# Queries and keys of three head pairs by seven products of halves, with residual tokens and finished heads kept in DRAM

## The chip, the core and the metric

The kernel runs on one core of a Trainium2 chip. A core has engines with instruction streams of their own: TensorE (PE) multiplies, VectorE (DVE) and ScalarE (ACT) work elementwise, GpSimd (POOL) and SyncE (SP) here mostly issue transfers. They meet through semaphores; each engine takes its instructions in the order in which the program has them. Matmul results land in PSUM banks of 2 KB per partition, everything else is in SBUF or DRAM. The metric is the device time of one execution in microseconds, here the median of the runs. The profiler took one execution in detail; its span (first to last instruction) is a little shorter than its measured time.

## The reference, cut to what matters

A model of two layers on 512 tokens of width 1024: dilated window attention and a SwiGLU block, then an mLSTM mixer and a SwiGLU block. The change touches the attention layer alone:

```python
def dilated_attention_mixer(xn, positions, w_in, w_out):
    proj = (xn @ w_in).reshape(B, S, N_GROUPS, 3, ATTN_HEADS, ATTN_HEAD_DIM)   # 3 groups, 8 heads of 128
    for g, (window, dilation) in enumerate(DIL_CONFIGS):                       # (128,1) (512,4) (2048,16)
        q = apply_partial_rope(proj[:, :, g, 0], positions) * scale            # rope on 32 of 128 features
        k = apply_partial_rope(proj[:, :, g, 1], positions)
        v = proj[:, :, g, 2]
        o, lse = dilated_window_attention(q, k, v, window, dilation)
    wts = jax.nn.softmax(jnp.stack(lses), axis=0)
    o = jnp.einsum('gbsh,gbshd->bshd', wts, jnp.stack(outs))
    return o.reshape(B, S, ATTN_WIDTH) @ w_out
```

All is fp32. With xn the normalised input, the queries and keys of one pair of heads in one group are xn times 2 x 256 columns of w_in.

## The kernel before

**Products.** TensorE multiplies in a rounded fp32 form, so each fp32 operand is split into a high part (rounded) and a low part (the rest), and each product is three matmuls: high by high, high by low, low by high (the list SPLITS). The normalised input lies in `pair[0]` (high) and `pair[1]` (low), eight tiles of 128 features by 512 tokens each.

**Weights.** A chunk of 4 x 128 rows by 256 columns (512 KB) is loaded on the SP queue into one of three "wraw" tiles; ACT writes its high part (line 210), DVE its low part (line 211), into three tiles each. `Feed` (line 263) keeps two chunks prepared ahead of the one that TensorE is using: `pop` hands out one and prepares the next of the list `plan`.

**Projections.** `project_pair` goes over groups g = 0, 1, 2 and over queries and keys. `project` (with `multiply`, line 241) gives each projection 48 matmuls 128x512: two chunks, two heads m, four k, three splits. ACT then copies 32 rows of the result to a `rot` tile (line 800) and the whole to the query or key tile (line 801). `rope` (lines 571 to 586) rotates the four 32-row parts at once on DVE (a shuffle, two products, a sum, each 128x512) and ACT copies them back (line 586).

**Attention.** The eight heads are four pairs, pr = 0 to 3. `attention_pair` makes scores of the first group (`scores0`, lines 642 and 648: masking and maxima on DVE, then exponentials on ACT, line 679), scores of the other two (`scores12`, lines 662 to 665, exponentials line 685), an exchange of maxima and sums across groups (lines 693 to 722, with one matmul, xps), the weighting of the probabilities (lines 730, 733, tensor-scalar on DVE), their transposes by DVE and a round trip to DRAM (line 739 and the tiles pD, pT; POOL queue), and the values (lines 757, 762), whose result ACT copies to `oT` (line 766), the tile "heads" with all eight heads.

**The order.** The work of one pair is laid over the projections of the next by ticks: `advance()` runs after each chunk, `defer(n, fn)` lets fn run n ticks later. RUN_AT = (2, (4, 5, 6, 7, 8), (10, 11), (2, 3, 1)) gives scores12 two ticks into the next pair, the exchange and first weighting at 4, transposes and the second weighting at 5 to 8, values at 10 and 11. So the weighting and transposes of pair pr-1 fall in the second group of pair pr, and the values in its third. `fenced()` and `run` hold the order on TensorE.

**Seven products, where they are already.** Most of the values, in the phase before pair 1, and the feed-forward compute a 2x2 block product with seven half-size products instead of eight (names P1 to P7, in the list ORDER: P1, P5, P2, P6, P7, P3, P4). It needs sums of operand blocks. The token sums S1 and S2 lie in the "heads" tile until the values phase ends, S3 and S4 in tiles of the values phase's own pool (`place`, freed with it). `sum_of` and `split_sum` make them. The residual tokens are the tiles `h` (tag "h"), to which `add_to_h` adds the output projection `awo`, the stage after the last values.

Of the kernel before, what the change touches and what calls it, by code (L numbers as in the profile page):

```python
# [72 lines left out]
def tile_hybrid_dilated_attn_mlstm(  # L73
# [310 lines left out]
    with ExitStack() as actx:  # L384
# [16 lines left out]
        posi = ap.tile([P, SEQ], I32, tag="rt", name="posi", bufs=2)  # L401
# [22 lines left out]
        def rope_tables():  # L424
# [142 lines left out]
        def rope(qk, rot, blocks, js=range(4), direct=False):  # L567

            at = slice(R * js[0], R * (js[-1] + 1))
# [3 lines left out]
            nc.vector.tensor_tensor(sh, sh, sinn[at], op=ALU.mult)  # L573
            if direct:
                for j in js:
                    mine = slice(R * j, R * (j + 1))
                    nc.vector.tensor_tensor(qk[j // 2][:R, j % 2], rot[mine, 0], rot[mine, 1], op=ALU.add)
                return
            nc.vector.tensor_tensor(a, a, sh, op=ALU.add)

            def back():
                for j in js:
# [3 lines left out]
                    nc.scalar.activation(t, part, AF.Copy)  # L586
            return back

        o_all = []

        def o_head(k):
            if not o_all:
                o_all.append(ap.tile([P, HEADS, SEQ], F32, tag="heads", name="oT"))
            return o_all[0][:, k]

        def attention_pair(pr, qks):
# [153 lines left out]
            def values(i, out=None):  # L750
# [30 lines left out]

        def project_pair(pr, qks, then=None):
            nm = "a%d" % pr
            for g in range(3):
# [4 lines left out]
                rot = ap.tile([P, 2, SEQ], F32, tag="rt", name="rot", bufs=2)  # L789
                for part in range(2):  # L790
                    t = tok_tile("%sg%d_%s" % (nm, g, "qk"[part]))

                    def evac(m, acc, t=t, rot=rot, g=g, part=part):
                        mine = rot[R * (2 * part + m):R * (2 * part + m + 1), 0]
                        views = (in_order, by_block) if g == 0 else (lambda x: x,) * 2
                        if pr == 0:
                            nc.vector.tensor_tensor(views[0](t[:, m]), views[1](acc), views[1](rbc), op=ALU.mult)
                            nc.scalar.activation(views[1](mine), views[0](t[:R, m]), AF.Copy)
# [1350 lines left out]
```

## Time and profile before

| | us |
|---|---|
| median of three runs | 1396.8 (1395.97 to 1398.32) |
| the profiled execution | 1396.37 |
| its span | 1394.5 |
| pair 2, first group (queries, keys, scores12 of pair 1 between) | 259.21 to 284.70 |
| pair 2, second group | 284.70 to 306.59 |
| pair 2, scores0, third group and values of pair 1 | 306.59 to 338.21 |
| pair 3, the same | 338.21 to 417.21 |
| values columns of pair 3, scores12, output projection, values of pair 3 | 417.21 to 495.25 |
| feed-forward of layer 0 starts | 495.25 |

The granted TensorE clock of the profiled execution is 0.999. In the lines shown below, a tile's name says where it belongs: a2g1k is pair 2, second group (g counts from 0), keys; `_w`, `_h`, `_l` are a raw chunk and its high and low parts; a1p the probabilities of pair 1; xa the normalised input; f0j the feed-forward of layer 0. Lines are those of the kernel before. A busy time counts instructions in execution, which overlap a little on DVE and ACT; so the distance between two starts is often shorter than one's length.

### The profile page before, as it was taken

What the parts mean: (1) busy time and instruction counts of PE and PEld (TensorE: products, weight loads), DVE (VectorE), ACT (ScalarE), POOL (GpSimd) and SP (SyncE); (2) the same over time, 40 slices, a digit from 0 to 9 for tenths busy, and PEclk for the clock granted to TensorE, in tenths of its full rate; (3) what the DMA queues carried; (4) which work ended last, traced back from release to release, by engine and by line L of the source; (5) the groups of instructions that cost most, each with busy time, mean ns of one, the idle gap of its engine ahead of it and who ended that gap; (6) DMA issues with size and microseconds to landing.
All of it is one profiled execution on the core that took longest, in us unless ns stands there. A gap on an engine that the chain in (4) does not pass through costs nothing. (4 is left out here: it accounts for less than half of the span.)

```text
span 1394.5 us, 21550 instructions
## 1 busy us (share of the span) xinstructions
PE 1379.0 (99%) x8308; PEld 1230.7 (88%) x8308; DVE 1046.9 (75%) x1781; ACT 777.2 (56%) x1280; POOL 156.9 (11%) x228
## 2 busy tenths in 40 slices
PE   9999999999999999999999999999999999999997
PEld 7888888888888889999999998897888899999886
DVE  7758746372638399877888898898858988888887
ACT  6546566455655255544576464785535554458854
POOL 2000011111111000000010110123201230001213
PEclk9999999999999999999999999999999999999999
DMA  7534256455453456233352743324334553335963
GB/s 240 164 121 137 78 166 204 121 161 150 126 169 105 159 146 169 95 122 121 108 157 69 175 115 91 92 76 121 91 119 111 142 181 121 122 110 132 197 166 99
DMA packets 137022, 186.39 MB, mean 134 GB/s; under 512 B 8628, under 2 KB 104436, under 8 KB 136920
## 3 DMA queue, kind: packets, MB, share of 16 engines
q1 hardware_dynamic: 117600, 136.14, 31.2%
q0 software_dynamic: 17664, 47.76, 15.0%
q8 instruction: 65, 1.06, 0.3%
q10 hardware_dynamic: 1656, 1.12, 0.2%
q14 instruction: 37, 0.30, 0.1%
HBM read 163.63 MB, written 18.87 MB: 131 GB/s over the span
## 5 line engine op out<-in xcount | busy, mean ns | idle before, releaser
L1452 POOL DMA_DIRECT2D f1T<-in_ffn_w_out_dram x15 | 17.8, 1186 | 208.7 <-DMA f1P_2w_w<-in_ffn_w_out_dram 136.2
L1427 POOL DMA_DIRECT2D f0S<-in_ffn_w_out_dram x10 | 8.7, 871 | 256.5 <-ACT f0P L1409 170.7
L1984 POOL DMA_DIRECT2D hD<-hB x32 | 21.8, 698 | 68.5 <-DVE hB L1981 68.5
L241 PE MATMUL mo<-n_h,mo_k_l 128*128 128x512 f32 x64 | 25.3, 395 | 0.0
L241 PE MATMUL mo<-n_h,mo_k_h 128*128 128x512 f32 x64 | 25.2, 394 | 0.0
L241 PE MATMUL mo<-n_l,mo_k_h 128*128 128x512 f32 x64 | 25.2, 393 | 0.0
L241 PE MATMUL mwo<-yo_l,mwo_k_h 128*128 128x512 f32 x64 | 25.1, 393 | 0.0
L241 PE MATMUL mqk<-n_h,mqk_k_h 128*128 128x512 f32 x64 | 25.1, 393 | 0.0
L241 PE MATMUL awo<-ao_h,awo_k_h 128*128 128x512 f32 x64 | 25.1, 392 | 0.0
L241 PE MATMUL mqk<-n_l,mqk_k_h 128*128 128x512 f32 x64 | 25.1, 392 | 0.0
L241 PE MATMUL f1j<-n_h,f1j_h 128*128 128x512 f32 x64 | 25.0, 391 | 0.0
L241 PE MATMUL f0j<-n_h,f0j_h 128*128 128x512 f32 x64 | 25.0, 391 | 0.0
L241 PE MATMUL mwo<-yo_h,mwo_k_l 128*128 128x512 f32 x64 | 25.0, 391 | 0.0
L241 PE MATMUL mqk<-n_h,mqk_k_l 128*128 128x512 f32 x64 | 25.0, 390 | 0.0
L241 PE MATMUL f0j<-n_h,f0j_l 128*128 128x512 f32 x64 | 24.9, 390 | 0.0
L241 PE MATMUL f1j<-n_h,f1j_l 128*128 128x512 f32 x64 | 24.9, 390 | 0.0
L241 PE MATMUL awo<-ao_h,awo_k_l 128*128 128x512 f32 x64 | 24.9, 389 | 0.0
L241 PE MATMUL f0j<-n_l,f0j_h 128*128 128x512 f32 x64 | 24.9, 389 | 0.0
L241 PE MATMUL f1j<-n_l,f1j_h 128*128 128x512 f32 x64 | 24.9, 389 | 0.0
L241 PE MATMUL awo<-ao_l,awo_k_h 128*128 128x512 f32 x64 | 24.9, 389 | 0.0
L241 PE MATMUL mwo<-yo_h,mwo_k_h 128*128 128x512 f32 x64 | 24.8, 391 | 0.0
L211 DVE TENSOR_TENSOR v1P_l<-v1W,v1P_h 128x1024 fp32r<-128x1024 f32 x14 | 17.1, 1223 | 9.6 <-ACT v1P_h L210 9.6
(2458 smaller groups left out, 5669.8 us busy)
## 6 DMA issues: line engine op xcount, KB each, us to landing
f0j_w<-in_ffn_w_in_dram SPq DMA_DIRECT2D x17, 512.0 KB, 6.0
f1j_w<-in_ffn_w_in_dram SPq DMA_DIRECT2D x17, 512.0 KB, 5.3
f1T<-in_ffn_w_out_dram POOLq DMA_DIRECT2D x15, 512.0 KB, 7.5
f0hid<-in_ffn_w_in_dram SPq DMA_DIRECT2D x9, 512.0 KB, 5.2
f1hid<-in_ffn_w_in_dram SPq DMA_DIRECT2D x9, 512.0 KB, 5.0
v0W<-in_attn_w_in_dram SPq DMA_DIRECT2D x8, 512.0 KB, 6.0
v1W<-in_attn_w_in_dram SPq DMA_DIRECT2D x8, 512.0 KB, 3.9
awo_k_w<-in_attn_w_out_dram SPq DMA_DIRECT2D x8, 512.0 KB, 3.9
```

The source lines that it names most:

```text
L211: nc.vector.tensor_tensor(lo[:, :n], raw[:, :n], hi[:, :n].bitcast(F32), op=ALU.subtract)
L241: nc.tensor.matmul(acc, whl[a][:, k, m * P:(m + 1) * P], pairs[b][kk], start=(kk == 0 and (a, b) == SPLITS[0]), stop=(kk == nk - 1 and (a, ...
L1427: nc.gpsimd.dma_start(t, src[1][:, ks], accum_op=ALU.add)
L1452: nc.gpsimd.dma_start(view(to), weight_rows(hk * UNITS + u, n), accum_op=ALU.add)
L1984: nc.gpsimd.dma_start(hD[k // 4].rearrange("(b i) x -> i b x", i=R)[:, :, c0:c0 + R], t[R * a_:R * (a_ + 1)])
```

## The change

For pairs 1 to 3 and the groups g = 1 and 2, six units in all, queries and keys together are one 2x2 block product: the halves of the 1024 features, the 256 query and 256 key columns, and the two halves of the tokens. With W11, W12, W21, W22 (feature half; 1 for queries, 2 for keys) and X00 to X11 (token half, feature half), the seven products are

```
P1 = W11 X00      P5 = (W12 - W11) S1          S1 = X10 + X11 blocks of the second token half
P2 = W21 X01      P6 = (W22 - W12 + W11) S2    S2 = S1 - X00
P3 = W22 S4       P7 = (W22 - W12) S3          S3 = X00 - X10
                  P4 = (W21 - W22 + W12 - W11) X11    S4 = X01 - S2
```

Each is 24 matmuls 128x256 (two heads, four k, three splits) against 96 matmuls 128x512 in a unit before. P1 and P2 give the queries of the first token half; u = P1 + P6 is kept (`vu`, with P5), P7 and then P4 are added on in the same bank; the key halves are a bank plus the part of `vu` (line 885 after the change, on DVE). The four weight blocks are loaded once per unit (`load_part`, W11 to a tile of its own), and their differences are made in place on DVE (`prepare_part`); each of the seven is split like any chunk.

So that the token sums live on through the attention layer, S3 and S4 move into the slots of the residual tokens h; these go to DRAM (`keep_tokens`, 8 x 256 KB, POOL queue) early in the kernel and come back (`bring_tokens`, SP queue) in the output projection. S1 and S2 stay in the slot of the heads; finished heads 0 to 5 go to DRAM one by one (`keep_head`) and come back in two loads (`bring_heads`) before the last values. The rope tile is laid out by token halves (its tables too), one tile instead of two; copies to and from it become half-size and twice as many where blocks or 256-token halves are moved.

```diff
-            for c in range(4):
-                s = slice(32 * c, 32 * c + 32)
-                nc.gpsimd.tensor_copy(sinn[:R, c * P:(c + 1) * P], sn[s])
-                nc.gpsimd.tensor_copy(cosn[:R, c * P:(c + 1) * P], cs[s])
-            for i in range(1, 4):
-                for t in (sinn, cosn):
-                    nc.gpsimd.dma_start(t[R * i:R * (i + 1)], t[:R])
+            for to, t in ((sinn, sn), (cosn, cs)):
+                for c in range(4):
+                    nc.gpsimd.tensor_copy(
+                        to[R * (c // 2):R * (c // 2 + 1)].rearrange("p (m s) -> p m s", m=2)[:, :, c % 2 * P:(c % 2 + 1) * P],
+                        t[R * c:R * (c + 1)].unsqueeze(1).to_broadcast([R, 2, P]))
+                nc.gpsimd.dma_start(to[2 * R:], to[:2 * R])
...
             def back():
-                for j in js:
-                    t, part = qk[j // 2][:R, j % 2], rot[R * j:R * (j + 1), 0]
+                for q in range(first, end):
                     if blocks:
-                        t, part = in_order(t), by_block(part)
-                    nc.scalar.activation(t, part, AF.Copy)
+                        for m in range(2):
+                            nc.scalar.activation(turned(qk, q, m, True), packed(rot, q, m, True), AF.Copy)
+                    else:
+                        nc.scalar.activation(halves(qk[q // 2][:R], q % 2), two_m(rot[quarter(q), 0]), AF.Copy)
...
+        oD = dp.tile([HEADS - 2, P, SEQ], F32, name="oD")
+        hD = dp.tile([KC, P, SEQ], F32, name="hD")
...
+        def keep_head(k, op):
+            t = npl.tile([P, SEQ], F32, tag="sq", name="o_keep", bufs=2)
+            nc.scalar.activation(t, op, AF.Copy)
+            nc.gpsimd.dma_start(oD[k], t)
+
+        def bring_heads():
+            t = ap.tile([P, HEADS - 2, SEQ], F32, tag="heads", name="oT")
+            o_all.append(t)
+            for ks in (slice(0, 4), slice(4, 6)):
+                nc.sync.dma_start(t[:, ks], oD[ks].rearrange("k p s -> p k s"))
+
+        def keep_tokens():
+            for k in range(KC):
+                nc.gpsimd.dma_start(hD[k], h[k])
+
+        def bring_tokens():
+            for k in range(KC):
+                h[k] = hp.tile([P, SEQ], F32, tag="h", name="h%d" % k, bufs=KC + 1)
+                nc.sync.dma_start(h[k], hD[k])
...
-                    nc.scalar.activation(o_head(2 * pr + i), op, AF.Copy)
+                    keep_head(2 * pr + i, op)
...
+        def load_part(pr, g, key):
+            if g > 2:
+                return
+            pool_, tag, bufs = (ap2, "wa", 1) if key == "W11" else (wp, "wraw", W_BUFS)
+            t = pool_.tile([P, 1024], F32, tag=tag, name="a%dg%d%s" % (pr, g, key), bufs=bufs)
+            k0, c0 = (int(key[1]) - 1) * 4 * P, g * 3 * D + (int(key[2]) - 1) * D + pr * 256
+            nc.sync.dma_start(four_k(t), w_in[k0:k0 + 4 * P, c0:c0 + 256].rearrange("(k p) n -> p k n", p=P))
+            parts_of.setdefault((pr, g), {})[key] = t
...
+        def prepare_part(pr, g, name):
+            b = parts_of[pr, g]
+
+            def less(out, x, y):
+                nc.vector.tensor_tensor(b[out], b[x], b[y], op=ALU.subtract)
+            src = {"P1": "W11", "P5": "W11", "P6": "W11", "P2": "W21", "P7": "W12", "P3": "W22", "P4": "W21"}[name]
+            if name == "P5":
+                less("W11", "W12", "W11")
+            elif name == "P6":
+                less("W11", "W22", "W11")
+            elif name == "P7":
+                less("W12", "W22", "W12")
+            whl = split_chunk((b[src], 1024, four_k, "a%dg%d%s" % (pr, g, name)))
+            if name == "P7":
+                less("W21", "W21", "W11")
+                for key in ("W11", "W12"):
+                    load_part(pr, g + 1, key)
+            elif name == "P4":
+                for key in ("W21", "W22"):
+                    load_part(pr, g + 1, key)
+            return whl
...
+        def qk_unit(pr, g, qk):
+            nm = "a%dg%d" % (pr, g)
+            last = pr == HEADS // 2 - 1 and g == 2
+            target = {"P1": "c11", "P2": "c11", "P5": "p5", "P3": "p5", "P6": "u", "P7": "u", "P4": "u"}
+            two_m = lambda t: t.rearrange("p (m s) -> p m s", m=2)
+            acc = {}
+            rot = vu = None
+
+            def pack(q, src):
+                nc.scalar.activation(two_m(rot[quarter(q), 0]), src, AF.Copy)
+
+            def finish(name):
+                nonlocal rot, vu
+                if name == "P1":
+                    acc["u"] = acc_tile(nm + "u")
+                    nc.scalar.activation(acc["u"], acc["c11"], AF.Copy)
+                elif name == "P5":
+                    vu = ap.tile([P, 2, SEQ], F32, tag="vu", name=nm + "vu")
+                    nc.scalar.activation(vu[:, 0], acc["p5"], AF.Copy)
+                elif name == "P6":
+                    nc.scalar.activation(vu[:, 1], acc["u"], AF.Copy)
+                elif name in ("P2", "P4"):
+                    th = int(name == "P4")
+                    src = two_m(acc[target[name]])
+                    if th == 0:
+                        rot = ap.tile([P, 2, SEQ], F32, tag="rot", name="rot")
+                    pack(th, src[:R])
+                    nc.scalar.activation(halves(qk[0], th), src, AF.Copy)
+                    if last and th:
+                        rope(qk, rot, False, 1, 2, True)
+                else:
+                    th = int(name == "P7")
+                    out = halves(qk[1], th)
+                    nc.vector.tensor_tensor(out, two_m(acc[target[name]]), two_m(vu[:, 1 - th]), op=ALU.add)
+                    pack(2 + th, out[:R])
+                    if last and th == 0:
+                        rope(qk, rot, False, 0, 1, True)
+                        rope(qk, rot, False, 2, 4, True)
+
+            for n, name in enumerate(ORDER):
+                key = target[name]
+                if name in ("P1", "P5"):
+                    acc[key] = acc_tile(nm + key)
+                whl = feed.pop()
+                with fenced():
+                    for m in range(2):
+                        for k in range(4):
+                            for a, b in SPLITS:
+                                if name in ("P1", "P2", "P4"):
+                                    x_ = pair[b][k + 4 * (name != "P1")][:, HALF * (name == "P4"):HALF * (1 + (name == "P4"))]
+                                else:
+                                    x_ = sum_part(name, b, k)
+                                nc.tensor.matmul(acc[key][:, m * HALF:(m + 1) * HALF], whl[a][:, k, m * P:(m + 1) * P], x_,
+                                                 start=(name in ("P1", "P5") and m == 0 and k == 0 and (a, b) == SPLITS[0]),
+                                                 stop=(m == 1 and k == 3 and (a, b) == SPLITS[-1]), skip_group_check=True)
+                finish(name)
+                if n == 6 and not last:
+                    defer(1, rope(qk, rot, False))
+                if n in (1, 3, 5, 6):
+                    advance()
...
+                if pr and g:
+                    qk.extend(tok_tile("%sg%d_%s" % (nm, g, "qk"[part])) for part in range(2))
+                    qk_unit(pr, g, qk)
+                    continue
...
+                        for th in range(2):
+                            q = 2 * part + th
+                            if pr == 0:
+                                nc.scalar.activation(packed(to, q, m, g == 0),
+                                                     turned((t, t), q, m, g == 0), AF.Copy)
+                            else:
+                                nc.scalar.activation(packed(to, q, m, False), acc[:R, th * HALF:(th + 1) * HALF], AF.Copy)
...
-            S[name] = ([heads_s[:, 2 * (int(name[1]) - 1) + i] for i in range(2)] if name in ("S1", "S2") else
-                       [place("s%d" % (2 * (name == "S4") + i), name + "hl"[i], (P, 4, HALF), F32R) for i in range(2)])
-            nc.scalar.activation(S[name][0], raw, AF.Copy)
-            nc.vector.tensor_tensor(S[name][1], raw, S[name][0].bitcast(F32), op=ALU.subtract)
+            if name in ("S1", "S2"):
+                hi, lo = (heads_s[:, 2 * (int(name[1]) - 1) + i] for i in range(2))
+                nc.scalar.activation(hi, raw, AF.Copy)
+                nc.vector.tensor_tensor(lo, raw, hi.bitcast(F32), op=ALU.subtract)
+                S[name] = [[t[:, k] for k in range(4)] for t in (hi, lo)]
+                return
+            S[name] = [[], []]
+            for i in range(2):
+                hi, lo = (hp.tile([P, 2, HALF], F32R, tag="h", name="%s%s%d" % (name, x, i), bufs=KC + 1) for x in "hl")
+                nc.scalar.activation(hi, raw[:, 2 * i:2 * i + 2], AF.Copy)
+                nc.vector.tensor_tensor(lo, raw[:, 2 * i:2 * i + 2], hi.bitcast(F32), op=ALU.subtract)
+                for a, t in enumerate((hi, lo)):
+                    S[name][a] += [t[:, k] for k in range(2)]
...
+            defer(1, keep_tokens)
...
-                if (pr, g) != (0, 0):
+                if pr and g:
+                    if (part, ch) == (0, 0):
+                        plan += [lambda pr=pr, g=g, name=name: prepare_part(pr, g, name) for name in ORDER]
+                elif pr and (part, ch) == (1, 1):
+                    plan.append(lambda pr=pr: last_plain(pr))
+                elif (pr, g) != (0, 0):
...
+        bring_heads()
...
+            if c == 2:
+                bring_tokens()
```

More of the change, by code (lines that the diff above doesn't have):

```diff
@@ L565, in tile_hybrid_dilated_attn_mlstm, with halves, turned, packed @@
         shift = [(k + 16) % 32 for k in range(32)]
-        def rope(qk, rot, blocks, js=range(4), direct=False):
-            at = slice(R * js[0], R * (js[-1] + 1))
+        quarter = lambda q: slice(R * q, R * (q + 1))
+        def halves(t, th):
+            return t[:, :, th * HALF:(th + 1) * HALF]
+        def turned(qk, q, m, blocks):
+            t = qk[q // 2][:R, m]
+            if blocks:
+                return in_order(t)[:, :, q % 2 * 2:(q % 2 + 1) * 2]
+            return t[:, q % 2 * HALF:(q % 2 + 1) * HALF]
+        def packed(rot, q, m, blocks):
+            a = rot[quarter(q), 0, m * HALF:(m + 1) * HALF]
+            return a.rearrange("p (c b j) -> p b c j", c=2, b=TB) if blocks else a
+        def rope(qk, rot, blocks, first=0, end=4, direct=False):
+            at = slice(R * first, R * end)
             a, sh = rot[at, 0], rot[at, 1]
@@ L793, in evac @@
                     def evac(m, acc, t=t, rot=rot, g=g, part=part):
-                        mine = rot[R * (2 * part + m):R * (2 * part + m + 1), 0]
+                        to = rot()
                         views = (in_order, by_block) if g == 0 else (lambda x: x,) * 2
@@ L812, in project_pair @@
                     qk.append(t)
-                    if pr == HEADS // 2 - 1 and g == 2:
-                        rope(qk, rot, False, (2 * part, 2 * part + 1), True)
-                    elif part == 1:
-                        turn = lambda qk=qk, rot=rot, g=g: rope(qk, rot, g == 0)
+                    if part == 1:
+                        turn = lambda qk=qk, rot=rot, g=g: rope(qk, rot(), g == 0)
                         if pr == 0 and g == 2:
```

36 lines of the change are left out of this document (23 added, 13 removed).

## The prediction

> **What bounds the kernel now.** I read the page first, then busy time by stretch, then single instructions of VectorE (DVE) and ScalarE (ACT) in one pair of heads. The profiled execution took 1396.37 us, its span is 1394.5, so 1.9 us lie around it; the runs' median is 1396.8, 0.4 above it.
>
> ```profile
> span 1394.5 us, 21550 instructions
> ...
> PE 1379.0 (99%) x8308; PEld 1230.7 (88%) x8308; DVE 1046.9 (75%) x1781; ACT 777.2 (56%) x1280; POOL 156.9 (11%) x228
> ...
> PE 26%; DVE 9%; ACT 2%; issue 1%; DMA 1%; ACTq 0%; DVEq 0%
> ```
>
> TensorE (PE) is busy 99% of the span, and the chain of waits names it most. So matmul time saved is saved for good, as long as DVE, at 75%, and ACT keep up. That is a question of single stages. The next view gives stretches of pair 2 (start and end in us): the second group (g1), the third group (g2) with the scores and values between, then the key projection of g1 alone, the query projection of g2, one half of the values, a piece of the feed-forward that already works with 128x256 products, and the start.
>
> ```profile
> core 0: us, PE busy (x) PEld busy (x) DVE busy (x) ACT busy (x) POOL busy (x), PEclk, DMA share, GB/s
> 284.70:306.59 21.89, 21.89 (x99) 18.11 (x98) 17.00 (x38) 11.42 (x18) 5.04 (x9) 1.00 0.61 176
> 306.59:338.21 31.62, 31.62 (x174) 27.45 (x172) 10.03 (x27) 16.19 (x35) 4.26 (x7) 1.00 0.58 182
> 295.71:306.59 10.88, 10.88 (x49) 9.01 (x48) 6.39 (x11) 4.50 (x7) 4.32 (x8) 1.00 0.93 261
> 320.56:323.83 3.27, 3.27 (x32) 3.27 (x30) 1.23 (x1) 2.21 (x3) 0.00 (x0) 1.00 0.53 160
> 540.21:700.00 159.79, 159.79 (x1331) 159.61 (x1330) 132.55 (x132) 79.48 (x97) 2.60 (x3) 1.00 0.38 116
> 309.44:320.56 11.12, 11.12 (x50) 9.18 (x49) 5.76 (x17) 8.30 (x24) 0.56 (x1) 1.00 0.57 207
> 8.60:56.80 48.20, 47.89 (x220) 38.79 (x221) 42.51 (x79) 31.05 (x54) 5.97 (x15) 1.00 0.60 185
> ```
>
> PE has no gap in any but the last, at the full clock. But in g1 DVE is busy 17.00 of 21.89 us, since the softmax work of the pair before (weighting, transposes) falls there; in g2 only 10.03 of 31.62.
>
> **The matmuls.** A projection is 48 matmuls 128x512 in 10.88 us, 226.7 ns each; a unit (queries and keys of one pair and group) has 96, 21.76 us. The new unit has 7 products of 24 matmuls 128x256. The feed-forward row gives 159.79 us / 1331 = 120.0 ns, so 2.88 us a product and 20.16 a unit. Gain 1.60 a unit, 9.6 us for six, if nothing waits.
>
> On this price the Trainium skill (TensorE: Matmul & The Clock Gate, section Back-to-back issue gap) gives N/2.4 + 2.5 ns for an isolated matmul, so 215.8 and 109.2, which by an estimate makes the gain 14.2 us; it also gives 131 ns for N=512 in a real stream, by which halves would lose. The trace disagrees with both (226.7 and 120.0), and the rows decide.
>
> **What the helpers get.** Per unit DVE makes 7 low parts instead of 4, 4 new differences of weight blocks, and 2 additions that finish the key halves out of PSUM; ACT makes 7 high parts instead of 4 and three more bank copies (P1's, P5's, P6's results). The DVE timeline of g1 (start, us, engine, line, operation), where it works without a gap:
>
> ```profile
> 285.68 1.23 DVE L211 TENSOR_TENSOR a2g1k_k_l<-a2g1k_k_w,a2g1k_k_h 128x1024 fp32r<-128x1024 f32 x1
> 286.82 0.17 DVE L714 TENSOR_TENSOR a1cf<-a1own,a1oth 128x16 f32<-128x16 f32 x1
> ...
> 289.19 0.69 DVE L579 TENSOR_TENSOR rot<-rot 128x512 f32<-128x512 f32 x1
> ...
> 290.29 1.08 DVE L730 TENSOR_SCALAR a1p<-a1p,a1cf 128x128 f32<-128x128 f32 x4
> ...
> 292.52 2.17 DVE L739 STREAM_TRANSPOSE a1pB<-a1p 128x1920 f32<-128x1920 f32 x1
> 294.62 1.19 DVE L211 TENSOR_TENSOR a2g1k_k_l<-a2g1k_k_w,a2g1k_k_h 128x1024 fp32r<-128x1024 f32 x1
> 295.72 0.87 DVE L730 TENSOR_SCALAR a1p<-a1p,a1cf 128x256 f32<-128x256 f32 x3
> ...
> 297.57 1.21 DVE L211 TENSOR_TENSOR a2g2q_k_l<-a2g2q_k_w,a2g2q_k_h 128x1024 fp32r<-128x1024 f32 x1
> ```
>
> From start to start: a low part 1.14 us (a difference has the same shape and engine, so I take 1.14; bounds 1.0 and 1.23, the row's own length), the rope and coefficients 2.37, the rope's sum with two small ones 1.10, weighting the first head 2.23, a transpose 2.10, weighting the second head 1.85. With 7 x 1.14 and two additions of 0.61 (a 128x512 operation: the rope's sum lasts 0.69, overlapped) the demand in g1 rises from 17.00 to 26.2 us, against 20.16 us of matmuls. Part of it can be done in g2, but each engine works in its written order. ACT's prices (line, engine, shapes, count, busy us, mean ns) over the pair, and the scores' reduction on DVE:
>
> ```profile
> L685 ACT ACTIVATE a1p<-a1p,a1nb 128x128 f32<-128x128 f32 x16 | 6.2, 389 | 2.3 <-DVE a1nb L674 2.3
> ...
> L679 ACT ACTIVATE a2p<-a2p,a2nb 128x256 f32<-128x256 f32 x6 | 3.0, 494 | 0.0
> L586 ACT ACTIVATE a2g_k<-rot 32x512 f32<-32x512 f32 x4 | 2.5, 630 | 0.1
> ...
> L210 ACT ACTIVATE a2g1k_k_h<-a2g1k_k_w 128x1024 fp32r<-128x1024 f32 x2 | 2.1, 1062 | 1.4 <-issue 1.3
> ...
> L801 ACT ACTIVATE a2g_k<-a2g1k 128x512 f32<-128x512 f32 x2 | 1.2, 598 | 0.0
> ...
> L800 ACT ACTIVATE rot<-a2g0k 32x512 f32<-32x512 f32 x2 | 1.2, 586 | 0.2
> ```
>
> ```profile
> L648 DVE CUSTOM_DVE_ANT_0 a2p<-a2s,acst 128x256 f32<-128x256 f32 x6 | 2.3, 418 | 0.0
> ```
>
> **The queue in g1, by the built order, on the clock of before.** PE runs P1, P5, P2, P6, four matmuls of P3, P7, the other twenty of P3, P4. P1 to P6 run from 284.70 to 296.2 in time. DVE, from 285.68: low part of P2 1.14, rope and coefficients 2.37, low part of P6 1.14, rope's sum 1.10, a difference 1.14, weighting 2.23, transpose 2.10, low parts of P7 and P3 2.28: 13.5 us, so 299.2, and about 0.3 later because P6's low part waits for its high part on ACT: 299.5. ACT, after the rope's sum (291.6 by the same list): eight copies back from the rope (32x256 now; 0.43 each by estimate, under the 0.63 of 32x512) 3.4, a bank copy 0.60, high part 1.06, pack and half copy 0.59 + 0.60, two high parts 2.12, P6's bank copy 0.60: 300.6. P7 adds into that same bank, so it starts at 300.7 and ends at 303.6; the twenty matmuls of P3 end at 306.0. P4 also waits for the key addition on DVE, behind the second weighting, P4's low part and the second transpose (299.5 + 1.85 + 1.14 + 2.10 + 0.6 = 305.2), so it runs 306.0 to 308.9. Before, g1 ended at 306.59: **+2.3 us**, a stall of 4.0 less the gain 1.6. Both engines reach P7 at the same time, so freeing one alone helps little. My ends are 1 us either way: +1.3 to +3.3.
>
> **The queue in g2.** The scores of the first group (309.44 - 306.59 = 2.85) end at 311.7, then P1, P5, P2 to 320.4. DVE, from 305.2: P1's low part, the second key addition, two differences, P5's low part (to 310.9), the rope with two of eight reductions (0.63 + 3 x 0.61 + 0.21 + 0.35, to 313.9), six reductions (0.35 apart, by estimate from the 418 ns with overlap) to 316.0, then P2's low part. ACT takes four rope copies (2.5) from 313.9, P1's bank copy 0.60 to 317.0, then the eight exponentials of these scores (2 x 0.389 + 6 x 0.494 = 3.7) to 320.7, and only behind them P6's high part, 321.8; its low part 322.9. So P6 starts at 323.0, a stall of 2.6. P7, P3, P4 (8.64) and the two halves of values (6.54) follow P6 (2.88): end 341.0 against 338.21, **+2.8 for the pair**. If P2's low part is late too, by up to 0.6, or g1 ends 0.4 later, +3.8. I take +3.2, a third of the way. Pairs 1 and 3 have the same stages and order; three pairs make **+9.6** (8.4 to 11.4).
>
> **Transfers and moves.** Weight loads keep their bytes, and what each load of g1 and g2 takes from issue to landing is:
>
> ```profile
> a2g1k_k_w<-in_attn_w_in_dram SPq DMA_DIRECT2D x2, 512.0 KB, 3.5
> a2g2q_k_w<-in_attn_w_in_dram SPq DMA_DIRECT2D x2, 512.0 KB, 3.5
> a2g2k_k_w<-in_attn_w_in_dram SPq DMA_DIRECT2D x2, 512.0 KB, 6.6
> ```
>
> The last two blocks of a unit are asked for at 300 to 303, behind the split of the unit before, and land by 309.3 at 6.6; DVE wants the first at about 308.3, and 1 us there is covered, since P5 starts on PE only at 314.6 with its low part ready at 310.9. The six head copies on ACT are the old copy (0.60) to another place; the store is issued by GpSimd (POOL), queued ahead of nothing due soon. The start issues 2 MB of token stores where the DMA queues are 0.60 busy at 185 GB/s: 11 us of transfer at that rate, spread over 40 us of room. Against it stand two table transfers instead of six. Each store of 256 KB is 1.4 us at that rate; nothing waits for it, and what it can hold up is the one load beside it: 0 to +1.4, and I take +0.3, near nothing, for most loads there are not waited for. At the end, two loads of heads (1.5 MB, waiting for P6 of the last unit, which frees their slot) and eight of tokens go on the SP queue ahead of weights; the output projection already waits once there:
>
> ```profile
> PE a3o L757 <- DMA a3pT<-a3pD: 1.9, 1, 1.9
> ```
>
> The heads are wanted about 30 us after they are asked for; I take 0, with -1 to +3 (the wait there may go, or more than double). Rope copies and packs in halves (four more a first group, 1.7 us of ACT, which is busy 777 of 1394.5) stand beside PE's work; uncovered they would cost that once per pair.
>
> **Sum:** 1396.4 + 9.6 + 0.3 = **1406.3 us**; with the bounds of its terms 1402 to 1411. That is 0.7% above the median.
>
> **Rivals.**
> *DVE and ACT keep up.* Each prepared product comes in time, as in the feed-forward, where DVE is busy 132.55 of 159.79 and PE never stops. For it: over a whole pair DVE has room, 17.00 + 10.03 of 53.5 us before in both groups. Against it: the order inside g1. Then -9.6, and in each g1 P7 follows P6 over the bank copy with only four matmuls (0.48) between (about 0.3 to reach ACT, 0.60, 0.1): +0.5, three times; 1396.4 - 9.6 + 1.5 + 0.3 = 1388.6. Chance 0.17.
> *Only g1 stalls.* If the exponentials in g2 go ahead of time, g2 keeps its gain: +2.3 - 1.6 a pair, so +2.1 and +0.3: 1398.8. Chance 0.15.
> *Slower by transfers too.* In g2 DVE's difference of two blocks stands ahead of P5's low part, so a late block holds DVE; it decides from 4 us later than 6.6. At 12 us it costs 1.4 per pair, 4.2, and the end up to 3: 1406.3 + 4.2 + 1.5 = 1412. For it: DMA is 0.93 busy in part of g1. Chance 0.11.
> *Matmuls at the isolated gap:* had halves and wholes the prices that need 14.2 instead of 9.6, all helpers in time, 1384; the two rows exclude it nearly. Chance 0.02. By the skill's page named above this is what would be.
>
> **How the numbers follow.** The forecast's case has 0.55. A measurement of this kernel tells 0.2%, 2.8 us, from no change: slower means above 1399.6. The forecast and the transfers lie there (0.66), of the case of g1 alone a third (0.05): slower 0.71. Same: the rest of that case (0.09). Faster: 0.17 + 0.02 and 0.01 of the case of g1 alone, 0.20. For 8 in 10 the range goes from 1387 to 1414; the likeliest case alone is 1402 to 1411.
>
> **What would show it.** Right: PE with waits in the four-matmul gap of P3 to P7 of g1 (for a copy on ACT or the low part of P3) of 3 to 5 us in each of pairs 1 to 3, and before P6 of g2 of 2 to 3.5 us (for P6's low part); DVE without a gap in g1; products of 2.88 us between; the first groups, values and feed-forward with their old lengths. Wrong: units of g1 near 20.2 us, or a wait on a transfer longer than 2 us, or a clock row under 1.00; or the output projection longer than before by over 3 us.

## The result, and the profile after

The changed kernel takes 1407.28 us in the median (1405.48 to 1408.34, four runs) against 1396.38 us before, a ratio of 1.0075 with a 95% interval of 1.0057 to 1.0092: 10.9 us slower, where 9.9 were forecast. The profiled execution took 1408.34 us with a span of 1406.6, so its span is 12.1 us longer than before. These lines of the page answer to those shown of before:

```profile
span 1406.6 us, 22635 instructions
...
PE 1375.8 (98%) x8740; PEld 1248.3 (89%) x8740; DVE 1104.5 (79%) x1841; ACT 802.5 (57%) x1346; POOL 163.8 (12%) x238
...
PE 27%; DVE 8%; ACT 2%; issue 1%; DMA 0%; ACTq 0%; DVEq 0%
```

TensorE is busy 3.2 us less than before, yet the span grew: the waits added more than the matmuls saved. The busy time by stretch says where. The rows are, for pairs 1, 2 and 3 in turn, the second group and then the scores of the first group, the third group and the values; the columns are those of the view before.

```profile
core 0: us, PE busy (x) PEld busy (x) DVE busy (x) ACT busy (x) POOL busy (x), PEclk, DMA share, GB/s
205.24:229.45 24.21, 22.24 (x172) 21.83 (x170) 22.64 (x45) 14.77 (x26) 4.93 (x9) 0.93 0.52 151
229.45:263.36 33.91, 31.75 (x247) 31.03 (x246) 19.60 (x36) 19.66 (x39) 4.03 (x7) 0.95 0.57 184
288.88:311.78 22.90, 20.93 (x171) 20.36 (x170) 22.41 (x44) 14.06 (x26) 4.51 (x9) 1.00 0.51 146
311.78:345.08 33.30, 30.64 (x246) 29.71 (x245) 19.65 (x36) 20.39 (x39) 4.43 (x8) 1.00 0.60 196
370.60:393.51 22.91, 20.94 (x171) 20.38 (x170) 22.41 (x44) 14.07 (x26) 4.73 (x9) 1.00 0.50 146
393.51:429.38 35.87, 32.15 (x246) 31.23 (x245) 25.55 (x47) 20.36 (x39) 4.09 (x8) 0.95 0.68 220
```

Before, these stretches took 21.89 and 31.62 us in each pair. The second groups are now 2.3, 1.0 and 1.0 us longer, the other stretches 2.3, 1.7 and 4.25. Together they lose 12.6 us, and the rest of the kernel (start, first groups, output projection, all behind it) changed by -0.5 in sum. In the second groups DVE is busy 22.4 of 22.9 us. In three of the six rows the granted clock is below 1.00, which it was in none of these stretches before.

The view of waits, TensorE's only (line, what it waited for, us in total, times, longest):

```profile
PE a3o L793 <- DMA a3pT<-a3pD: 2.4, 1, 2.4
PE a2g2u L904 <- ACT a2g2P_h L210: 1.7, 1, 1.7
PE a3g2u L904 <- ACT a3g2P_h L210: 1.7, 1, 1.7
...
PE a1g2u L904 <- ACT a1g2P_h L210: 1.4, 1, 1.4
PE a3g2c L904 <- ACT a3g2u L867: 1.3, 1, 1.3
PE a2g1p L904 <- ACT a2g1P_h L210: 1.1, 1, 1.1
...
PE a2g1p L904 <- DVE a2g1P_l L211: 0.9, 1, 0.9
...
PE a2g2u L904 <- DVE a2g2P_l L211: 0.8, 1, 0.8
```

In each name, g1 or g2 is the group and the last letter the bank: p is P5's and P3's, u is P6's, P7's and P4's, c is P1's and P2's. So each second group waits 1.1 us for P3's high part and 0.9 for its low part, where 3 to 5 were forecast in this place, and each third group up to 1.7 us for P6's high part and 0.8 for its low part, as forecast; pair 3 also waits 1.3 us before P2. The longest wait, 2.4 us for the last transposed probabilities, was 1.9 before. Of the first kind, DVE's timeline of the second group of pair 2:

```profile
289.85 1.23 DVE L211 TENSOR_TENSOR a2g1P_l<-a2g1W,a2g1P_h 128x1024 fp32r<-128x1024 f32 x1
...
295.26 1.22 DVE L834 TENSOR_TENSOR a2g1W<-a2g1W,a2g1W 128x1024 f32<-128x1024 f32 x1
296.39 1.07 DVE L766 TENSOR_SCALAR a1p<-a1p,a1cf 128x128 f32<-128x128 f32 x4
...
298.62 2.18 DVE L775 STREAM_TRANSPOSE a1pB<-a1p 128x1920 f32<-128x1920 f32 x1
300.72 2.32 DVE L211 TENSOR_TENSOR a2g1P_l<-a2g1W,a2g1P_h 128x1024 fp32r<-128x1024 f32 x2
302.95 0.96 DVE L766 TENSOR_SCALAR a1p<-a1p,a1cf 128x256 f32<-128x256 f32 x3
...
308.11 0.65 DVE L885 TENSOR_TENSOR a2g_k<-a2g1u,a2g1vu 128x512 f32<-128x512 f32 x1
```

DVE works from 289.85 to 308.7 without a gap, on the list of the prediction: the difference takes 1.13 us to the next start, as taken there, and the low parts of P7 and P3 are done at 302.95, 14.1 us after the group's start (forecast 14.8). ACT in the same group and in the third one:

```profile
295.30 1.16 ACT L600 ACTIVATE a2g_q<-rot 32x256 f32<-32x256 f32 x3 [1.64 <-DVE rot L594]
...
300.65 1.99 ACT L210 ACTIVATE a2g1P_h<-a2g1W 128x1024 fp32r<-128x1024 f32 x2
302.54 0.57 ACT L872 ACTIVATE a2g1vu<-a2g1u 128x512 f32<-128x512 f32 x1
...
317.86 1.28 ACT L602 ACTIVATE a2g_q<-rot 32x512 f32<-32x512 f32 x2 [2.88 <-DVE rot L594]
...
320.33 0.57 ACT L867 ACTIVATE a2g2u<-a2g2c 128x512 f32<-128x512 f32 x1
320.93 0.40 ACT L715 ACTIVATE a2p<-a2p,a2nb 128x128 f32<-128x128 f32 x1
...
324.67 1.04 ACT L210 ACTIVATE a2g2P_h<-a2g2W 128x1024 fp32r<-128x1024 f32 x1
```

ACT waits for the rope's sum on DVE (295.30), then has no gap until P3's high part (300.65) and P6's bank copy, done 14.2 us after the group's start (forecast 15.9). In the third group the rope's copies start at 317.86, P1's bank copy at 320.33, the eight exponentials run to 324.67, and P6's high part stands behind them. The rope's copies are late because DVE comes late to the rope. It waits for a weight block of the unit first, 0.86 us in pair 2 and 1.92 in pair 3:

```profile
312.48 1.23 DVE L834 TENSOR_TENSOR a2g2W<-a2g2W,a2g2W 128x1024 f32<-128x1024 f32 x1 [0.86 <-DMA a2g2W<-in_attn_w_in_dram]
...
314.77 0.73 DVE L585 STREAM_SHUFFLE rot<-rot 128x512 f32<-128x512 f32 x1
...
395.27 1.23 DVE L834 TENSOR_TENSOR a3g2W<-a3g2W,a3g2W 128x1024 f32<-128x1024 f32 x1 [1.92 <-DMA a3g2W<-in_attn_w_in_dram]
```

The second kind of loss was not forecast. This view has P7 in pair 1 and P7 in pair 2, 24 matmuls each (the clock is the third column from the end):

```profile
219.82:224.17 4.35, 4.35 (x27) 4.35 (x25) 4.35 (x8) 0.00 (x0) 0.00 (x0) 0.61 0.98 259
303.43:306.30 2.87, 2.87 (x26) 2.87 (x25) 2.87 (x8) 0.00 (x0) 0.00 (x0) 1.00 0.95 191
```

Both follow the same two waits. Behind them, pair 1 goes at a clock of 0.61 and takes 1.5 us longer; pair 2 does not. P6 of the third group is as slow in pairs 1 and 3 (5.36 and 5.27 us with its second wait, against 4.00 in pair 2). The three make 1.48 + 1.36 + 1.27 = 4.1 of the 12.6 us.

### The profile page after: what moved, and what is told of

Same layout as the page of the kernel before. It is cut to its first block, busy times and chain, and to the rows that moved or that the text cites. A ratio compares the mean times of both kernels' runs of the same rounds, so it can differ in the third digit from the quotient of the medians.

```text
span 1406.6 us, 22635 instructions
## 1 busy us (share of the span) xinstructions
PE 1375.8 (98%) x8740; PEld 1248.3 (89%) x8740; DVE 1104.5 (79%) x1841; ACT 802.5 (57%) x1346; POOL 163.8 (12%) x238
```

## The experiments

**The moves alone.** All of the change but the seven products.

```diff
+SEVEN = ()
-                if pr and g:
+                if (pr, g) in SEVEN:
                     qk_unit(pr, g, qk)
```

> All of the change but the seven products: sums on chip, tokens and heads through DRAM, new rope layout, while queries and keys of all groups are the plain 96 matmuls 128x512. Theory (the time is lost at the seven products): the moves cost nothing that can be measured, 1396.4 within 1 us (ratio 0.9993 to 1.0007), and the output projection starts as far behind the last values columns as before. Rival (the DRAM round trips cost): 1400 or more (ratio 1.0025 or more), with PE waiting for a transfer of tokens or heads.

Measured: 1396.35 us, ratio 1.0002 (0.9993 to 1.0011). The moves cost nothing that can be measured, by this interval at most 1.5 us; the loss comes from the products.

**One group alone.** The same edit with the units of the second group, SEVEN = ((1, 1), (2, 1), (3, 1)), the run g1_only, and with those of the third, ((1, 2), (2, 2), (3, 2)), the run g2_only.

> Seven products in the second group of pairs 1 to 3 only, the third group plain. Theory (DVE and ACT are late for P3 and P7 because the weighting and transposes of the pair before fall there): each second group is about 1.0 us longer than before, 2.3 where the granted clock falls after the waits; 1396.4 + 3.0 to 4.3 = 1399.4 to 1400.7 (ratio 1.002 to 1.003). Rival (the loss arises in the third group and only shows in both): the second groups gain, 1391.6 to 1394.

Measured: 1402.42 us (1398.66 to 1403.05), ratio 1.0039 (1.0026 to 1.0051). It stays slow, so the loss starts in the second group. The range of the theory was missed by 1.7 us: it had room for one slow clock, and two of the three groups met one. The second groups take 22.9, 24.2 and 24.2 us; this is P7 of pairs 1 and 2 in this run:

```profile
219.84:222.72 2.88, 2.88 (x27) 2.88 (x26) 2.88 (x8) 0.00 (x0) 0.00 (x0) 1.00 0.91 182
299.85:304.22 4.37, 4.37 (x27) 4.37 (x26) 4.37 (x8) 0.00 (x0) 0.00 (x0) 0.61 0.97 256
```

Here pair 1 keeps the clock and pairs 2 and 3 lose it, behind waits that are the same to 0.1 us. The executions of this kernel show it too: 1398.66 and 1399.92 us at a mean clock of 0.997, 1402.42 to 1403.05 at 0.994 and 0.995. The changed kernel's four are 1405.48 at 0.999, 1406.55 and 1408.01 at 0.997, 1408.34 at 0.994.

> Seven products in the third group of pairs 1 to 3 only, the second group plain. Theory (the third group's waits before P2 and P6 are late work of DVE and ACT handed on from the second group): without it the waits vanish, three units gain 1.6 each, 1391.6 to 1393 (ratio 0.9965 to 0.9976). Rival (the exponentials of the scores ahead of P6's high part make the wait by themselves): the third groups stay 1 us or more longer than before, 1399 or more.

Measured: 1392.74 us, ratio 0.9975 (0.9966 to 0.9984), inside what the theory gave. In pair 2, the third group and the values without the scores:

```profile
307.70:335.08 27.38, 27.27 (x230) 27.04 (x229) 14.18 (x28) 17.14 (x35) 4.03 (x7) 1.00 0.59 194
```

With the scores it is 30.23 us against 31.62, a gain of 1.4 a unit. The exponentials stand ahead of P1's bank copy here, but they start 4.7 us after the scores do (309.54 and 304.85 in its trace) where it is 9.2 in the changed kernel (320.93 and 311.78), because DVE comes to the reductions in time. So they hurt the third group only when DVE is late from the second. Against the same runs of before (1396.1), the second groups alone make +6.3 us and the third alone -3.4, together about +3; the changed kernel is 10.9 slower, so some 8 us arise only where the two follow one another.

**Filling the waits.** Matmuls that nobody reads, to keep TensorE going.

```diff
+                if (g, name) in JUNK:        # (1, "P6"): 20, (2, "P2"): 24
+                    run(lambda: [nc.tensor.matmul(junk[:, :HALF], whl[0][:, 0, :P], x_, start=True, stop=True)
+                                 for _ in range(JUNK[g, name])])
```

> The changed kernel with idle matmuls that nobody reads: 20 of 128x256 behind P6 in each second group and 24 behind P2 in each third group (2.4 and 2.9 us), where TensorE waits anyway. Theory (the granted clock falls after the waits, and matmuls at 213 instead of 120 ns cost about 4 us in pairs 1 and 3): the clock stays at 1.00, and the time falls by 2 to 4 us to 1403 to 1405, though TensorE does 132 matmuls more. Rival (the slow matmuls have another cause, or the idle matmuls come on top): 1407 or more.

Measured: 1426.53 us, ratio 1.0218. As a test of the total it failed: with the added matmuls, their fences and their bank, ACT's instructions were built in another order, the eight exponentials came ahead of P1's bank copy, and P2 waited 4.7 to 6.2 us for it in every third group. Its second groups were filled as meant and kept the clock at 1.00 in all three pairs, at 23.1 us. The test was repeated there alone:

> The run named g1_only (1402.4 us) with 20 idle matmuls 128x256 that nobody reads, 2.4 us, behind P6 of each second group, where TensorE waited 1.1 and 0.9 us and where in pairs 2 and 3 of that run P7 went at 213 instead of 120 ns a matmul. Theory (a short wait lets the granted clock fall, and the slow matmuls cost 1.5 us each time): with the wait filled the clock stays at 1.00 in the second groups, each is 23.1 us long as in the run named filled, and the time falls by 1.5 to 3 us, 1399.4 to 1401, with 60 matmuls more. Rival (the slow matmuls come from something else): P7 still goes at 213 ns somewhere and the time is 1402 or more.

Measured: 1402.29 us, ratio 1.0043 (1.0029 to 1.0057), the time of the run without filling. The row of pair 2's second group:

```profile
285.81:308.91 23.10, 22.85 (x192) 22.68 (x191) 20.01 (x42) 13.26 (x24) 4.57 (x9) 1.00 0.51 144
```

The first half of the expectation held: no second group is slow (23.1 us each, 1.1 less than the two slow ones), and three of five executions have a mean clock of 0.999 (0.994 to 0.997 without filling); the other two have 0.996 and 0.997. The time did not follow, and the rival's number came without its cause, since in pair 3 the stretch behind it grew from 31.6 to 34.7 us: the key projection now waits 1.8 us for the query's bank copy, behind exponentials that ACT reaches later. In the two profiles with filling none of six second groups is slow, against seven of twelve in four profiles without. So the waits bring the slow clock, which costs 1.3 to 1.5 us each time; that filling them pays is not shown.

**The differences elsewhere.** `nc.gpsimd` for `nc.vector` in the weight differences of `prepare_part`.

> The changed kernel with the four weight differences of each unit on GpSimd instead of DVE: DVE has 4.6 us less to do in each unit. Theory (in the second group ACT's queue reaches P7's condition at the same time as DVE reaches P3's, so freeing DVE alone gains little there; the third group gains the 2 to 3 us by which the rope comes earlier): 1401 to 1405 (ratio 1.003 to 1.006). Rival (DVE's load alone makes the waits): all waits go, 1389 or less. Second rival (GpSimd takes far longer than DVE for a difference, over 3 us, and the products wait for it): 1407 or more.

Measured: 1437.22 us, ratio 1.0297 (1.0281 to 1.0312): the second rival's time, though its condition, a difference of over 3 us, did not come. From GpSimd's and DVE's timelines in the third group of pair 2:

```profile
323.75 5.17 POOL L834 TENSOR_TENSOR a2g2W<-a2g2W,a2g2W 128x1024 f32<-128x1024 f32 x2
```

```profile
326.61 2.87 DVE L587 TENSOR_TENSOR rot<-rot,sinn 128x512 f32<-128x512 f32 x1
```

A difference takes 2.6 us on GpSimd, behind the stores of transposed probabilities in its queue. The DVE product that meets it takes 2.87 us instead of 0.68. And the built order of ACT now has P5's high part behind the exponentials, so that a difference ready at 328.9 is taken up at 337.3; P5 waits 7 to 8 us for it. What freeing DVE would give is not answered by this run.

**Earlier weighting.** RUN_AT gets the scores, the exchange and all behind it one tick earlier (the run early); then the same with the scores left in place; then the first with the differences on GpSimd.

```diff
-RUN_AT = (2, (4, 5, 6, 7, 8), (10, 11), (2, 3, 1))
+RUN_AT = (1, (3, 4, 5, 6, 7), (10, 11), (2, 3, 1))
```

> The changed kernel with the scores of the second and third groups, the exchange, both weightings and transposes of the pair before one tick (one weight chunk of the plain first group, 5.4 us) earlier; nothing else. Theory (the waits are a matter of the order of DVE and ACT work in the second group): weighting and first transpose move into the first group where DVE has idle time, P3 and P7 come in time, the third group is as short as where the second was plain: 1388 to 1392 (ratio 0.994 to 0.997). Rival (DVE or ACT has too much to do over the pair as a whole): the waits move elsewhere, 1400 or more. Second rival (the scores then wait for the rope of the pair before): PE waits 1 us or more before the scores, 1393 to 1397.

Measured: 1426.05 us, ratio 1.0219. The theory failed. The first rival's number came and the waits moved elsewhere, but that the helpers have too much to do over the pair as a whole is not shown by it. Two of TensorE's waits:

```profile
PE a2g2c L904 <- ACT a2g2u L867: 3.8, 1, 3.8
PE a2g1u L904 <- DVE a2g1P_l L211: 2.6, 1, 2.6
```

The products of pair 2's second group run from 296.8 to 322.7 here, and DVE has one gap, of 0.9 us, from 290.3 to 315.9: the weighting and first transpose now stand ahead of P6's low part, 2.6 us late, and in the third group the exponentials stand ahead of P1's copy. A tick of 5.4 us moves the wait in pairs 2 and 3 from P3 to P6 in the second group and from P6 to P2 in the third.

> As in the run named early, but the scores stay where they are; only the exchange and what follows it come one tick earlier. Theory: the exchange's matmul now waits for the exponentials (6.2 us of ACT behind the scores) by 1 to 3 us per pair, and the second group is in time: 1393 to 1400. Rival (the exponentials are done by then): as early, 1388 to 1392.

Measured: 1432.08 us, ratio 1.0255. The exchange's matmul waited 4.5 us for the sums of the exponentials, more than the 1 to 3 forecast, and the second groups were not in time either (waits of 1.0 to 1.1 and 0.8 us at P3):

```profile
PE a1xps L734 <- DVE a1ex L729: 4.5, 1, 4.5
```

> Both: one tick earlier, and the differences on GpSimd. Theory (order was the cause, load is not): within 2 us of the run named early. Rival (DVE's load is what is left): 3 us or more faster than early.

Measured: 1473.03 us, ratio 1.0554, slower than either; the high part of P5 is waited for 10 to 12 us in each third group. Neither reading of the expectation came true, since the high parts stand behind the exponentials again.

**The exponentials out of the third group** (the run scores0_late).

```diff
-defer(SCORES0_AT, lambda: run(fn))
+defer(8 if pr < HEADS // 2 - 1 else 4, lambda: run(fn))
```

> The changed kernel with the first group's scores of pairs 1 and 2, and so their reductions and exponentials, moved behind the third group to the start of the next pair; pair 3 keeps its place. Theory (the third group waits at P6 because the eight exponentials, 3.7 us, stand ahead of P6's high part on ACT): in pairs 1 and 2 the third group with the values takes 27 to 28 us without the scores (20.2 + 6.5 and little else), 2 to 3 us less per pair than the changed kernel, the second groups stay near 22.9; pair 3 as in the changed kernel. 1400 to 1403. Rival (DVE's and ACT's load is the same, so the wait moves on): 1406 or more.

Measured: 1412.46 us, ratio 1.0111: the theory's time failed and the rival's came. The wait at P6 is gone in pairs 1 and 2, and stays in pair 3, so in this order the exponentials cause it. But the third group then reaches its second half of values sooner than the transposed probabilities come back from DRAM, and that wait takes its place (3.6 us in pair 1, 3.2 in pair 2):

```profile
PE a0o L793 <- DMA a0pT<-a0pD: 3.6, 1, 3.6
PE a1o L793 <- DMA a1pT<-a1pD: 3.2, 1, 3.2
...
PE a3g2u L904 <- ACT a3g2P_h L210: 1.7, 1, 1.7
```

**No differences at all**, on top of that (the call in `prepare_part` does nothing).

> As scores0_late, but with the four weight differences of each unit left out, so that P4 to P7 multiply by plain weight blocks and the queries and keys of those groups are not the reference's; DVE has 4.6 us less to do per unit and nothing else changes. Theory of the prediction (ACT reaches P7's condition when DVE reaches P3's): the second groups are shorter by 0.5 us at most, 22.4 to 22.9. Rival (the differences on DVE are the whole reason): the second groups fall to 20.3 to 21 us, and the time by 5 us or more against scores0_late.

Measured: 1413.79 us, ratio 1.0110 (1.0090 to 1.0129), no faster than with them. P3 in the second group of pair 2 waits as it did:

```profile
300.91 0.38 PE L904 MATMUL a2g1p<-S4h,a2g1P_h 128*128 128x256 f32 x1 [1.11 <-ACT a2g1P_h L210]
...
302.17 0.39 PE L904 MATMUL a2g1p<-S4h,a2g1P_l 128*128 128x256 f32 x1 [0.76 <-DVE a2g1P_l L211]
```

The group takes 24.1 us, of which P7 loses 1.3 to the clock, so 22.8; pair 1's, at full clock, takes 22.6. Taking 4.6 us of work from DVE shortens the group by 0.1 to 0.3, inside what the theory gave. In this trace ACT waits for the rope's sum (294.48) and then has no gap until P3's high part and P6's bank copy, done at 302.3, and P3's low part on DVE stands behind that high part: ACT's chain alone is long enough for the wait. What freeing ACT, or both, would give was not run.

**A version faster than the kernel before and the changed one.** The third groups alone, and 12 matmuls of the output projection moved ahead of the last values.

```diff
             out_part(i, whl[i], 1, (0, 1))
+            if i == 0:
+                out_part(2, whl[2], 1, (0, 1))
             run(lambda: last_values(i, head_split))
-        out_part(2, whl[2], 1, (0, 1))
```

> The run named g2_only (1392.7 us) with 12 matmuls of the output projection (third pair of columns, first two heads) moved ahead of the last values, where TensorE waits 2.6 us for the transposed probabilities and then goes at 213 ns for about 20 matmuls. Theory (the wait and the slow clock behind it are filled by 2.7 us of work): 2 to 4 us less, 1388.7 to 1390.7 (ratio 0.995). Rival (the transposed probabilities only come that much later, or the work moved away uncovers another wait): 1392 or more.

Measured: 1388.97 us (1388.69 to 1389.39), ratio 0.9947 (0.9934 to 0.9960). The stretch from the values columns of pair 3 to the feed-forward:

```profile
412.64:489.38 76.74, 76.17 (x384) 64.49 (x383) 45.34 (x110) 34.01 (x72) 4.38 (x8) 1.00 0.55 168
```

It was 78.04 us before, 78.52 in the changed kernel and 80.37 with the third groups alone. The wait for the last transposed probabilities falls to 0.6 us, and the clock stays up behind it.

## Why the prediction was right, point by point

*The sign and the sum.* Forecast 1406.3, measured 1407.28. The sign follows from the mechanism; that the numbers lie 1 us apart is luck, for three errors of 3 to 4 us, not all of one sign, stand in the sum. Over the three pairs the second groups were to lose 6.9 us and lost 2.9 at full clock, the third groups were to lose 2.7 and lost 5.6, and the slow clock took 4.1 that the sum did not have. Two sums of the prediction are off without deciding anything: DVE's list in the third group adds up to 310.4, not 310.9, and the bounds of the terms to 1403.8 to 1412.2, not 1402 to 1411.

*The matmuls.* Right: a product is 2.88 us where nothing waits, and with the third groups alone a unit gains 1.4 of the 1.60.

*The second group.* The mechanism was right and the size too large: +2.3 forecast, +1.0 measured at full clock. The term is ACT's chain to P6's bank copy, 1.7 us too long. Of this, 0.5 is the rope's sum on DVE, which came 6.4 us after the group's start and not 6.9; the other 1.2 is that I had taken each instruction's length (0.60 for a bank copy, 0.43 for a half copy of the rope) where the distance from start to start counts (0.48 and 0.38), the same overlap that I had used for DVE. DVE's list was 0.7 too long, so the two chains end within 0.1 us of one another, and the trace puts TensorE's waits on P3's two parts and none on the bank copy. That freeing DVE alone helps little was borne out: without the differences the group is 0.1 to 0.3 shorter.

*The third group.* The order that makes P6 wait was right, and moving the exponentials away removed the wait. Its size was too small: +0.5 forecast, 0.9 with the third of the way that I added; at full clock it was 0.9, 1.7 and 3.0 in pairs 1 to 3. One step failed: I had written that a late weight block is covered because P5 is in time. The block was 0.86 us late in pair 2, near the 1 us forecast, and P5 was in time, but the rope stands behind it on DVE, its copies and P1's bank copy behind that on ACT, and so P6 and in pair 3 P2 too. That P2 adds into P1's bank and so waits for this copy, I had not priced at all (0.2 us in pair 2, 1.3 in pair 3). Pair 3 loses most; its block is 1.92 us late, 1.1 more than in pair 2, and its wait before P2 is 1.1 longer.

*The clock.* Missing from the sum. I named a clock under 1.00 as a thing that would prove the argument wrong, and it did drop, for 4.1 us of 12.6; it is not another cause but a consequence of the waits, and it goes with them (1.00 in these stretches with the third groups alone). The waits lose time without it too: the changed kernel's execution at a mean clock of 0.999 has a span of 1402.1 us, 7.6 longer than the profiled one of before.

*Moves and transfers.* +0.3 forecast; the moves alone give 1.0002, nothing that can be measured. The output projection's stretch grew by 0.5, as near to 0 as forecast; the wait of 2.4 us in it is over the 2 us that I had named as a sign against the argument, but was 1.9 before.

*The rivals.* That DVE and ACT keep up is right for the third groups and wrong for the second: over both groups DVE has room, inside the second it has none. That only the second group stalls did not happen: the stall was handed on to the third. A weight block over 4 us late did not come; one 1.92 us late already cost something, in pair 3, by the way of the rope. The matmuls at the isolated gap are excluded by the 2.88 us of a product.

So of 12.6 us, 8.5 are waits less the matmul gain (9.6 forecast) and 4.1 the clock behind them.

## What to carry to other kernels

Before cheaper matmuls are bought with more work on the helpers, add up the helpers' list inside the very stage where it lands, in the built order: with the same edit, the stage where DVE was busy 10 of 32 us gained when it was changed alone, the one with 17 of 22 lost, and where both were changed the loss moved on to the neighbour. Price a queue by distances from start to start. Small shifts of such a full queue moved the wait and changed the built order behind it; putting the new work only where there is room, and filling the one long wait with work that was there anyway, gave 0.9947.

## What the runs showed of the hardware

The clock fell behind short waits. Two waits of 1.1 and 0.8 to 0.9 us within 3 us were followed by it in seven of the twelve second groups of four runs (the changed kernel, the second groups alone, the late scores, no differences), not in the others, and then about 16 matmuls went at 213 instead of 120 ns.

The clock records in the traces show where. Each slow stretch is 3.41 us long or a multiple of that, and within a trace all of them start on one grid of 3.41 us. In the changed kernel the two waits of pair 1 lie in the first of the windows below and the second window is slow; those of pair 2 are shared by the third and the fourth (columns as in the views above, so PE's busy time stands behind the comma):

```profile
216.35:219.76 3.41, 1.44 (x10) 1.03 (x9) 3.41 (x5) 3.13 (x5) 2.18 (x4) 1.00 0.36 72
219.76:223.17 3.41, 3.41 (x18) 3.41 (x17) 3.41 (x9) 0.00 (x0) 0.00 (x0) 0.50 0.92 214
298.27:301.68 3.41, 2.35 (x20) 2.15 (x18) 3.41 (x4) 3.38 (x7) 0.59 (x2) 1.00 0.35 121
301.68:305.09 3.41, 2.50 (x18) 2.29 (x19) 3.41 (x10) 1.43 (x3) 1.59 (x3) 1.00 0.86 140
```

TensorE is busy 42% of the first window, and 69% and 73% of the other two. Over the fourteen traces, their starts and ends left out, the clock fell from full to half 48 times, each time after a window of the grid in which TensorE was busy 53% or less; the least busy window without a fall had 48%. So the same 2 us of waits cost 1.5 us or nothing, by where they lie on the grid, and the grid lies otherwise in each trace. This is read from the traces; no run moved a wait on purpose to test it.

The Trainium skill (TensorE: Matmul & The Clock Gate, section What's actually happening) has a free-running window of 3.4 us whose activity sets the clock, half or full: the half clock and the slow stretches of 3.41 us agree with it. The same section of the Trainium skill states an idle window of that length as the condition; here a window that was half busy was enough.

A GpSimd subtraction of 128x1024 took 2.4 to 2.9 us against 1.13 from start to start on DVE, and a DVE product of two operands beside it 2.87 instead of 0.68. The Trainium skill (SBUF — State Buffer, section Who interferes with whom) has a DVE instruction with two SBUF inputs contend with a GpSimd instruction that reads SBUF; the row agrees, with 2.2 us more.
